# A fifth load buffer, loads in halves, a sum of squares in PSUM and branch products beside the last head in a one-core transformer block

## The chip, the cores and the metric

The kernel runs on one core of one Trainium2 chip. The metric is the device time of one execution in microseconds (us): for the kernel before, the median of three runs is 3460.16 us, from 3459.18 to 3461.2. The profile comes from one execution of 3459.31 us, whose span on the core is 3457.6 us.

Engine names: PE is TensorE (matmul), PEld its weight load, DVE VectorE, ACT ScalarE, POOL GpSimd, SP SyncE, which here issues DMAs.

## The reference, cut to what matters

One layer for 512 tokens (plus 16 meta tokens) of width 2048, in float32:

```
h  = rmsnorm(x)
x += (sigmoid(gate_a) * (MLA(h) @ w_a) + sigmoid(gate_b) * (StickBreaking(h) @ w_b)) @ w_out
x += PEER(rmsnorm(x))       # 128 x 128 experts, 8 heads, 16 experts a head and token
out = rmsnorm(x)
PEER, for one token:  act = gate * gelu(u[idx] . x);   y = sum over idx of act * v[idx]
```

MLA and stick-breaking have eight heads of width 128 each. The expert tables u and v have 16384 rows of 2048.

## The kernel before, in words

**Products.** A float32 product is made of three matmuls of split operands (`mm3`, L258 to L261): low weight by high value, high weight by low value, high by high. A weight block of 128 x 1024 goes through `wtile` (L232): SP loads it to a raw tile `wr` (L243), ACT copies it to `wh` (L245), DVE subtracts to get `wl` (L246), then 24 matmuls use both. Values are split the same way by `split` (L263): ACT copies (L264), DVE subtracts (L265). There are 4 raw buffers (`raw_half`, L229) and 3 pairs of `wh` and `wl`, in the output stage a fourth pair in a pool of its own (`weights_v`). A raw buffer is free again when its block's subtraction has ended, a pair when the block's matmuls have.

**Stages.** The front projections and stick-breaking attention fill the first 800 us. Then come the MLA heads, about 800 to 961 us: for each head h, generators are run in turn (`run`, L787), one step of each at a time: scores and softmax of head h+1 (`mla_s`, L724), projections of head h+2 (`mla_p`, L708) and the value product of head h (`mla_y`, L760). In `mla_y`, PE transposes the probabilities `pt` (L772), ACT and DVE split the transposes into `th` and `tl_`, and PE multiplies them with the values (L781 to L783). Beside the last head, h = 7, there is nothing else to run. The branch merge follows (loop over 16 chunks m): for `wa` and for `wb` a block is loaded and multiplied into one PSUM bank (24 matmuls of 128 x 512), then gated by a sigmoid (L836, L837) and added. Before the loop, the stick-breaking result `yb` is split into `yh_b` and `yl_b`.

**PEER.** 328 of the 512 tokens (ND) are computed densely, over all experts; the other 184 gather rows of u and v with indirect DMAs from POOL, and DVE multiplies (L1065) and accumulates (L1073) these rows, one row instruction of 128 x 2048 each. The u stage runs from about 1550 to 2488 us, and its activations go to memory (`h_d`, `g_d`). The output stage runs from about 2488 to 3440 us: it multiplies 256 blocks of v (`vb`), 128 x 1024 each, with the gated activations. The experts form NG = 32 groups of GRP = 4. The work goes in 33 steps i (STEPS), the first of 5 blocks, then of 8 (the last of 3); a step uses the groups i-1 and i. qi counts the blocks within a step.

**Activations of a group** arrive by two loads on SP, `hin` (L1327, 656 KB) and `gin` (L1319, 672 KB); each tile tag has two buffers. `gated` (L1333) multiplies them on DVE (L1337, L1339), at qi = QM = 3 of the step before they are used; `group_split` (L1406) splits the product into `vah` (ACT) and `val` (DVE, L265), at qi = 5 (4 in step 0). Right behind the split, `group_in` (L1324) issues both loads for the group after the next. SP takes its instructions in order; so a load whose buffer isn't free holds up the loads of weights behind it.

**What sets the order.** Each engine runs its instructions in the order in which the program gives them, after a scheduler that places them by their dependencies. By `follows` (L1330) the gated product stays behind the newest weight subtraction; the row instructions are spread by a pace (L1502).

**The end.** As each of the 16 chunks c of the output is complete (accumulated at L1498 and L1500), `fin_add` (L1417) squares it on ACT (L1420) and adds the square to `ssf` on DVE (L1422). `fin_out` (L1424) then sums over partitions by one matmul with ones (L301), makes 1/sqrt of it (`rstd`, L309 to L315: ACT ln, DVE scale, ACT exp, four DVE instructions), scales the 16 chunks (L1429) and issues 8 output DMAs (L1431). It is called once for the columns past 328, in the last step, and once at the very end for the first 328.

Of the kernel before, what the change touches and what calls it, by code (L numbers as in the profile page):

```python
# [2 lines left out]

# [20 lines left out]
P = 128  # L24
# [27 lines left out]
QM, QS = 3, 5  # L52
# [163 lines left out]
def body(tc, nc, a, dbg=None):  # L216
# [12 lines left out]
    def raw_half():  # L229
        return wp.tile([P, 1024], F32, name="wr", tag="wr", bufs=4)  # L230
# [568 lines left out]
    run(mla_s(0), mla_p(1))  # L799
    for h in range(H):  # L800
        if h == 1:
            mla_r(1)
        if h in (2, 3):
            mla_rope(h)
        if h == 4:
            values(1)
        run(*([mla_s(h + 1)] if h + 1 < H else []), *([mla_p(h + 2)] if h + 2 < H else []), mla_y(h))
# [18 lines left out]
    for m in range(KC):  # L826
        acc = []
        for name, yh_, yl_, gi in (("wa", *ys[0], 0), ("wb", *ys[1], 1)):
            gt = sp2.tile([P, SEQ], F32, name="g2", bufs=4)
            SP.dma_start(gt, gates[gi, m])  # L830
            wh, wl = front(name, m)
            ps = ps_tile()
            for k in range(8):
                s = slice(k * P, (k + 1) * P)
                mm3(ps, wh[:, s], wl[:, s], yh_[:, k], yl_[:, k], k == 0, k == 7)
# [479 lines left out]

    def group_g(g):
        gt = vi.tile([P, D], F32, name="gin", tag="gin")[:, :NBT * GRP * TH]
        gt = gt.rearrange("p (b j t) -> p b j t", j=GRP, t=TH)
        SP.dma_start(gt, g_d[g])  # L1319
        return gt  # L1320
# [3 lines left out]
    def group_in(g):  # L1324
        if g not in held:
            ht = hin_tile()
            SP.dma_start(ht, h_d[g])  # L1327
            held[g] = [ht, group_g(g)]

# [85 lines left out]
    rf = ap2.tile([P, SEQ], F32, name="rf")  # L1415

    def fin_add(c, t0, t1, first):  # L1417
        t = slice(t0, t1)
        sq = ssf if first else vp.tile([P, SEQ], F32, name="fsq", bufs=1)
        S.activation(sq[:, t], acc[:, c, t], AF.Square)  # L1420
        if not first:
            V.tensor_add(ssf[:, t], ssf[:, t], sq[:, t])  # L1422

    def fin_out(t0, t1):  # L1424
        sc = vp.tile([P, D], F32, name="sc", tag="row", bufs=1).rearrange("p (k t) -> p k t", t=SEQ)
        rstd(rf[:, t0:t1], ssf[:, t0:t1], t1 - t0, D, [sc[:, k] for k in range(3)], None)
        for c0, n in ((0, 1), (1, 2), (3, 3), (6, 3), (9, 3), (12, 2), (14, 1), (15, 1)):
# [3 lines left out]
            SP.dma_start(a["out"][c0:c0 + n, :, t0:t1].rearrange("k p t -> p k t"), acc[:, c0:c0 + n, t0:t1])  # L1431

# [8 lines left out]
    for i, step in enumerate(STEPS):  # L1441
# [11 lines left out]
        for qi, (g, q8) in enumerate(step):  # L1453
            wh, wl = wtile(a["vb"][at])
            at += 1
            if i + 1 < NG and qi == QM:
                gated(*held[i + 1])
# [21 lines left out]
            if i + 1 < NG and qi == (QS if i else 4):  # L1479
                group_split(i + 1)  # L1480
                if i + 2 < NG:
                    group_in(i + 2)
            for dc in range(2):
# [20 lines left out]
                if i >= NG - 1 and not stays:  # L1504
                    fin_add(c, 0, ND, not done)
# [4 lines left out]
    fin_out(0, ND)  # L1510
# [19 lines left out]
```

## Time and profile before

| what | value |
|---|---|
| time, median of three runs | 3460.16 us (3459.18 to 3461.2) |
| time of the profiled execution | 3459.31 us |
| its span on the core | 3457.6 us |
| PE busy | 3420.5 us, 99% |
| PEld busy | 3188.2 us, 92% |
| DVE busy | 2573.5 us, 74% |
| ACT busy | 1427.4 us, 41% |
| POOL busy | 776.1 us, 22% |
| moved by DMA | 919.94 MB, mean 266 GB/s |
| mean granted TensorE clock | 0.995 |

Busy shares are averages over stages of different kinds. A matmul's shown duration is longer than its share of the time, since matmuls are pipelined: how long one takes in a stream is read from the count in a window. "[1.79 <-DVE wl L246]" behind a row of a timeline says that the engine stood idle for 1.79 us before this instruction and that the last thing it waited for was the DVE instruction of L246 that wrote `wl`. In the table by windows, the clock is the share of full speed that was granted to TensorE, and the DMA share is the mean busy share of the core's 16 DMA engines.

### The profile page before, as it was taken

The numbers are of one execution on the slowest core, as the hardware profiler recorded it, in microseconds if no ns is written. First come the engines' busy times: TensorE is split into PE (matmuls) and PEld (weight loads), VectorE is DVE, ScalarE is ACT, GpSimd is POOL, SyncE is SP. The second block draws the span as 40 slices with busy tenths as digits, with TensorE's granted clock in tenths as the row PEclk, the third lists the DMA queues.
The fourth block names the chain that finished last, engine by engine and source line by source line (L and its number), as shares of the span: only waits on it lengthen the run. The fifth ranks groups of instructions, "written<-read, shape, count | busy, mean of one in ns | idle before, by whom it ended". The sixth has DMA issues, their size and how long they took to land.

```text
span 3457.6 us, 53380 instructions
## 1 busy us (share of the span) xinstructions
PE 3420.5 (99%) x21115; PEld 3188.2 (92%) x21115; DVE 2573.5 (74%) x3573; ACT 1427.4 (41%) x2304; POOL 776.1 (22%) x555
## 2 busy tenths in 40 slices
PE   9999999999999999999999999999999999999997
PEld 8988888887888888889999999999999999999997
DVE  5533334445754557999999988887889999999997
ACT  4233333334543223223576776774333333333333
POOL 1000000000001113322333333333213333333320
PEclk9999999999999999999999999999999999999998
DMA  5322323232144345559999999999999999999993
GB/s 171 100 98 100 98 100 100 89 101 74 62 131 143 129 143 181 204 214 367 377 389 407 405 412 412 405 401 398 403 362 375 394 408 400 402 382 399 409 381 116
DMA packets 227141, 919.94 MB, mean 266 GB/s; under 512 B 27806, under 2 KB 53518, under 8 KB 179090
## 3 DMA queue, kind: packets, MB, share of 16 engines
q1 hardware_dynamic: 134660, 466.11, 36.6%
q0 software_dynamic: 60480, 411.68, 30.0%
q10 hardware_dynamic: 31750, 38.75, 3.1%
q8 instruction: 165, 2.70, 0.3%
q14 instruction: 86, 0.70, 0.1%
HBM read 854.57 MB, written 62.91 MB: 265 GB/s over the span
## 4 chain that ended last, share of the span: by engine, by line
PE 81%; DVE 11%; DMA 4%; issue 2%; ACT 1%; SPq 0%; POOL 0%; DVEq 0%; ACTq 0%
PE ps L259 26%; PE ps L260 25%; PE ps L261 25%; DMA wr<-vb 3%; DVE wl L246 3%; DVE xg L1073 1%; DVE row L1065 1%; PE ps L1252 1%; DVE acc L1073 1%; DVE acc L1500 1%; DVE hgl L246 0%; ACT wh L245 0%; DVE hin L1337 0%; DMA row<-u,eo 0%; DVE acc L1429 0%
## 5 line engine op out<-in xcount | busy, mean ns | idle before, releaser
L245 ACT ACTIVATE wh<-wr 128x1024 fp32r<-128x1024 f32 (+1 forms) x654 | 687.8, 1053 | 1402.6 <-PE ps L261 1038.7
L246 DVE TENSOR_TENSOR wl<-wr,wh 128x1024 fp32r<-128x1024 f32 (+1 forms) x639 | 812.0, 1279 | 391.5 <-ACT wh L245 389.3
L259 PE MATMUL ps<-vah,wl 128*128 128x328 f32 x2048 | 643.8, 314 | 7.0 <-DVE wl L246 6.8
L260 PE MATMUL ps<-val,wh 128*128 128x328 f32 x2048 | 642.7, 314 | 0.0
L261 PE MATMUL ps<-vah,wh 128*128 128x328 f32 x2048 | 639.7, 312 | 0.0
L259 PE MATMUL ps<-hgh,wl 128*128 128x328 f32 (+1 forms) x1488 | 490.9, 330 | 2.8 <-DVE wl L246 2.8
L261 PE MATMUL ps<-hgh,wh 128*128 128x328 f32 (+1 forms) x1488 | 486.1, 327 | 0.0
L260 PE MATMUL ps<-hgl,wh 128*128 128x328 f32 (+1 forms) x1488 | 485.8, 326 | 0.0
L259 PE MATMUL ps<-xh,wl 128*128 128x512 f32 (+1 forms) x1376 | 468.1, 340 | 1.5 <-ACT xh L366 1.5
L260 PE MATMUL ps<-xl,wh 128*128 128x512 f32 (+1 forms) x1376 | 465.0, 338 | 0.8 <-DVE xl L367 0.8
L261 PE MATMUL ps<-xh,wh 128*128 128x512 f32 (+1 forms) x1376 | 464.9, 338 | 0.0
L259 PEld LDWEIGHTS ps<-vah,wl 128*128 128x128 f32 x2048 | 386.3, 189 | 9.5 <-DVE wl L246 9.3
L260 PEld LDWEIGHTS ps<-val,wh 128*128 128x128 f32 x2048 | 387.1, 189 | 0.0
L261 PEld LDWEIGHTS ps<-vah,wh 128*128 128x128 f32 x2048 | 386.8, 189 | 0.0
L1052 POOL DMA_INDIRECT row<-v,eo x128 | 215.5, 1684 | 481.4 <-DVE xg L1073 414.4
L1073 DVE SCALAR_TENSOR_TENSOR xg<-row,act,xg 128x2048 f32<-128x2048 f32 x127 | 297.5, 2343 | 1.2 <-DMA row<-v,eo 1.1
L1065 DVE SCALAR_TENSOR_TENSOR row<-row,xg 128x2048 f32<-128x2048 f32 x128 | 292.1, 2282 | 4.8 <-DMA row<-u,eo 4.8
L259 PEld LDWEIGHTS ps<-hgh,wl 128*128 128x128 f32 x1488 | 280.1, 188 | 14.6 <-DVE wl L246 3.4
L261 PEld LDWEIGHTS ps<-hgh,wh 128*128 128x128 f32 x1488 | 280.1, 188 | 11.7 <-issue 0.2
L260 PEld LDWEIGHTS ps<-hgl,wh 128*128 128x128 f32 x1488 | 280.4, 188 | 10.9
L259 PEld LDWEIGHTS ps<-xh,wl 128*128 128x128 f32 x1376 | 258.6, 188 | 30.2 <-ACT xh L366 3.0
L260 PEld LDWEIGHTS ps<-xl,wh 128*128 128x128 f32 x1376 | 259.1, 188 | 29.1 <-DVE xl L367 1.7
(517 smaller groups left out, 6057.6 us busy)
## 6 DMA issues: line engine op xcount, KB each, us to landing
wr<-ut SPq DMA_DIRECT2D x256, 512.0 KB, 9.4
wr<-vb SPq DMA_DIRECT2D x256, 512.0 KB, 8.0
wr<-front SPq DMA_DIRECT2D x238, 512.0 KB, 3.3
g_d<-gb POOLq DMA_DIRECT2D x42, 512.0 KB, 10.9
gin<-g_d SPq DMA_DIRECT2D x32, 672.0 KB, 7.4
h_d<-hb ACTq DMA_DIRECT2D x128, 164.0 KB, 8.3
hin<-h_d SPq DMA_DIRECT2D x32, 656.0 KB, 8.9
gates<-gt ACTq DMA_DIRECT2D x32, 256.0 KB, 2.0
```

Source lines behind the costliest of these rows:

```text
L245: more["last"] = S.activation(hi[:, s], r, AF.Copy)
L246: sub = (eng or V).tensor_sub(lo[:, s], r, hi[:, s].bitcast(F32))
L259: T.matmul(ps, wl, xh, start=start, stop=False)
L260: T.matmul(ps, wh, xl, start=False, stop=False)
L261: T.matmul(ps, wh, xh, start=False, stop=stop)
L1052: G.indirect_dma_start(out=row, out_offset=None, in_=a[src], in_offset=bass.IndirectOffsetOnAxis(ap=eos[part][:, k:k + 1], axis=0))
L1065: ins = V.scalar_tensor_tensor(row, row, 1.0, xs[part], ALU.mult, ALU.mult, accum_out=w)
L1073: ins = V.scalar_tensor_tensor(y, row, w, y, ALU.mult, ALU.add)
L1252: T.matmul(bank[:, o:o + P], ohs[q % 4][:, 1, :, t], wos[:, q % 4, c, :, t], start=c == 1, stop=c == 0)
L1500: mark = V.tensor_add(acc[:, c, :ND], acc[:, c, :ND], ps[:, :ND])
```

## The change

Four parts.

- **A fifth raw buffer** in the output stage: every fifth `wr` tile comes from the pool `weights_v`. Room is made by putting `rf` into a fourth part of the scratch tile `sc`, and by making the tile of squares 328 wide, in two buffers, rather than 512 wide in one.
- **Activation loads in four halves.** Groups 0 and 1 are loaded as before. For groups from 2 on, `group_part` issues one of four loads at each of the blocks qi = 0 to 3 (1 to 4 in step 1) of the step before the group is used: two of `hin` (two of the four experts each, 128 x 656) and two of `gin` (128 x 640 and 128 x 704). The gated product is at qi = 3, 5, 4 in steps 0, 1 and from 2 on, the split at 4, 6, 5. Whole loads for the group after the next, behind the split, are gone.
- **The last square in PSUM.** `fin_last` sums, in one PSUM bank, `ssf` of the first 15 chunks and then the square of the last chunk, by two matmuls with ones; `fin_end` makes the root with three DVE instructions behind the exp rather than four, and sends the output by 10 DMAs rather than 8.
- **Branch products beside the last heads.** `branch_ahead` splits `yb` into tiles of its own (8 splits, beside head 6) and makes the `wb` products for m = 0, 1, 2 beside heads 6 and 7, two k at a step. The merge loop takes these banks when it comes to them. The splits into `yh_b` and `yl_b` stay as well.

```diff
-QM, QS = 3, 5
+QM, QS = 4, 5
...
     def raw_half():
+        if more["pool"] is not None and more["n"] % 5 == 0:
+            return more["pool"].tile([P, 1024], F32, name="wr", tag="wr")
         return wp.tile([P, 1024], F32, name="wr", tag="wr", bufs=4)
 
...
+    AHEAD = 3
+    ready = {}
+
+    def branch_ahead():
+        bh, bl = ([lp.tile([P, 4, n], F32R, name=x, tag=t)[:, :, :SEQ] for t, n in ((f"cq{p}", SEQ), (f"ck{p}", LEN))]
+                  for x, p in (("ybh", "h"), ("ybl", "l")))
+        for h in range(H):
+            split(bh[h // 4][:, h % 4], bl[h // 4][:, h % 4], yb[:, h])
+            yield
+        for m in range(AHEAD):
+            wh, wl = front("wb", m)
+            ps = ready[m] = ps_tile()
+            for k in range(8):
+                s = slice(k * P, (k + 1) * P)
+                mm3(ps, wh[:, s], wl[:, s], bh[k // 4][:, k % 4], bl[k // 4][:, k % 4], k == 0, k == 7)
+                if k % 2:
+                    yield
+
...
-        run(*([mla_s(h + 1)] if h + 1 < H else []), *([mla_p(h + 2)] if h + 2 < H else []), mla_y(h))
+        if h == H - 2:
+            ahead = branch_ahead()
+        run(*([mla_s(h + 1)] if h + 1 < H else []), *([mla_p(h + 2)] if h + 2 < H else []), mla_y(h),
+            *([ahead] if h == H - 1 else [islice(ahead, 9)] if h == H - 2 else []))
...
-            wh, wl = front(name, m)
-            ps = ps_tile()
-            for k in range(8):
-                s = slice(k * P, (k + 1) * P)
-                mm3(ps, wh[:, s], wl[:, s], yh_[:, k], yl_[:, k], k == 0, k == 7)
+            if gi and m in ready:
+                ps = ready.pop(m)
+            else:
+                wh, wl = front(name, m)
+                ps = ps_tile()
+                for k in range(8):
+                    s = slice(k * P, (k + 1) * P)
+                    mm3(ps, wh[:, s], wl[:, s], yh_[:, k], yl_[:, k], k == 0, k == 7)
...
+    def group_part(g, k):
+        if k == 0:
+            held[g] = [hin_tile(), gin_tile()]
+        ht, gt = held[g]
+        j, b = slice(k * GRP // 2, (k + 1) * GRP // 2), slice((k - 2) * NBT // 2, (k - 1) * NBT // 2)
+        ld = SP.dma_start(ht[:, j], h_d[g][:, j]) if k < 2 else SP.dma_start(gt[:, b], g_d[g][:, b])
+        tc.add_manual_dep(ld.ins, more["last"].ins.name, NOSYNC, reason="keeps the loads spread")
 
...
-    rf = ap2.tile([P, SEQ], F32, name="rf")
 
     def fin_add(c, t0, t1, first):
         t = slice(t0, t1)
-        sq = ssf if first else vp.tile([P, SEQ], F32, name="fsq", bufs=1)
-        S.activation(sq[:, t], acc[:, c, t], AF.Square)
+        sq = ssf[:, t] if first else vp.tile([P, ND], F32, name="fsq", bufs=2)[:, :t1 - t0]
+        S.activation(sq, acc[:, c, t], AF.Square)
         if not first:
-            V.tensor_add(ssf[:, t], ssf[:, t], sq[:, t])
+            V.tensor_add(ssf[:, t], ssf[:, t], sq)
 
...
+        rf = sc[:, 3]
...
+    final = {}
+
+    def fin_last(c):
+        ps = final["ps"] = ps_tile()
+        T.matmul(ps[:, :ND], ones, ssf[:, :ND], start=True, stop=False)
+        sq = vp.tile([P, ND], F32, name="fsq", bufs=2)
+        S.activation(sq, acc[:, c, :ND], AF.Square)
+        T.matmul(ps[:, :ND], ones, sq, start=False, stop=True)
+
+    def fin_end():
+        sc = vp.tile([P, D], F32, name="sc", tag="row", bufs=1).rearrange("p (k t) -> p k t", t=SEQ)
+        v, r0, t, rf = (sc[:, k, :ND] for k in range(4))
+        ps = final["ps"][:, :ND]
+        S.activation(t, ps, AF.Ln, scale=1.0 / D, bias=C("eps"))
+        V.tensor_scalar(v, ps, 1.0 / D, EPS, ALU.mult, ALU.add)
+        S.activation(r0, t, AF.Exp, scale=-0.5)
+        V.tensor_mul(v, v, r0)
+        V.scalar_tensor_tensor(v, v, -0.5, r0, ALU.mult, ALU.mult)
+        V.scalar_tensor_tensor(rf, v, 1.5, r0, ALU.add, ALU.mult)
+        for c0, n in ((0, 1), (1, 1), (2, 2), (4, 2), (6, 2), (8, 2), (10, 2), (12, 2), (14, 1), (15, 1)):
+            for c in range(c0, c0 + n):
+                V.scalar_tensor_tensor(acc[:, c, :ND], acc[:, c, :ND], gain("fin")[:, c:c + 1],
+                                       rf, ALU.mult, ALU.mult)
+            SP.dma_start(a["out"][c0:c0 + n, :, :ND].rearrange("k p t -> p k t"), acc[:, c0:c0 + n, :ND])
 
...
-            if i + 1 < NG and qi == QM:
+            if 1 <= i < NG - 1:
+                for k in ({k + (i == 1): (k,) for k in range(4)}).get(qi, ()):
+                    group_part(i + 1, k)
+            if i + 1 < NG and qi == (3, 5, QM)[min(i, 2)]:
                 gated(*held[i + 1])
...
-            if i + 1 < NG and qi == (QS if i else 4):
+            if i + 1 < NG and qi == (4, 6, QS)[min(i, 2)]:
                 group_split(i + 1)
-                if i + 2 < NG:
-                    group_in(i + 2)
...
-                    fin_add(c, 0, ND, not done)
+                    if len(done) == KC - 1:
+                        fin_last(c)
+                    else:
+                        fin_add(c, 0, ND, not done)
                     done.append(c)
...
-    fin_out(0, ND)
+    fin_end()
```

How it moves instructions, at three places. Line numbers of the changed kernel differ: L249 is the weight subtraction there (L246 before), L1365 the load of a half, L1375 and L1377 the gated product, L1562 and L1564 the accumulation, L1100 the row instruction, L268 the split on DVE.

First SP's queue at the start of the output stage, where the loads of `vb` blocks (`wr`) begin. Before:

```order
145 L243 DMA wr<-vb 128x1024 x7
146 L1395 DMA select<-select 128x56
147 L243 DMA wr<-vb 128x1024
148 L1319 DMA gin<-g_d 128x1344
149 L243 DMA wr<-vb 128x1024
150 L1327 DMA hin<-h_d 128x1312
151 L243 DMA wr<-vb 128x1024 x4
152 L1319 DMA gin<-g_d 128x1344
153 L243 DMA wr<-vb 128x1024 x2
154 L1327 DMA hin<-h_d 128x1312
155 L243 DMA wr<-vb 128x1024
156 L1327 DMA hin<-h_d 128x1312
```

And of the changed kernel:

```order
143 L246 DMA wr<-vb 128x1024 x7
144 L1433 DMA select<-select 128x56
145 L246 DMA wr<-vb 128x1024 x3
146 L1365 DMA hin<-h_d 128x656 x2
147 L1365 DMA gin<-g_d 128x640
148 L246 DMA wr<-vb 128x1024 x3
149 L1365 DMA gin<-g_d 128x704
150 L246 DMA wr<-vb 128x1024 x4
151 L1365 DMA hin<-h_d 128x656 x2
152 L246 DMA wr<-vb 128x1024
153 L1365 DMA gin<-g_d 128x640
154 L246 DMA wr<-vb 128x1024
```

Seven weight loads come before `select` in both. Behind it, one weight load and then a whole `gin` and `hin` stood between the blocks, each with one block; now three weight loads come first, and the halves stand between them.

Second, DVE at the same place, from the first subtractions for `vb` blocks (`wl`) on. Before:

```order
2036 L246 TENSOR_TENSOR wl<-wr,wh 128x1024 x4
2037 L1498 COPY acc<-ps 128x328
2038 L1071 TENSOR_SCALAR acc<-row,actb 128x16x128
2039 L1498 COPY acc<-ps 128x328
2040 L1337 TENSOR_TENSOR hin<-hin,gin 128x20x4x16
2041 L1498 COPY acc<-ps 128x328
2042 L1339 TENSOR_TENSOR hin<-hin,gin 128x4x8
2043 L246 TENSOR_TENSOR wl<-wr,wh 128x1024
2044 L1498 COPY acc<-ps 128x328
2045 L1073 SCALAR_TENSOR_TENSOR acc<-row,actb,acc 128x16x128
2046 L1498 COPY acc<-ps 128x328 x2
2047 L1073 SCALAR_TENSOR_TENSOR acc<-row,actb,acc 128x16x128
```

And of the changed kernel:

```order
2041 L249 TENSOR_TENSOR wl<-wr,wh 128x1024 x3
2042 L1562 COPY acc<-ps 128x328
2043 L1098 TENSOR_SCALAR acc<-row,actb 128x16x128
2044 L1562 COPY acc<-ps 128x328
2045 L249 TENSOR_TENSOR wl<-wr,wh 128x1024
2046 L1562 COPY acc<-ps 128x328
2047 L249 TENSOR_TENSOR wl<-wr,wh 128x1024
2048 L1562 COPY acc<-ps 128x328
2049 L1100 SCALAR_TENSOR_TENSOR acc<-row,actb,acc 128x16x128
2050 L1562 COPY acc<-ps 128x328
2051 L1375 TENSOR_TENSOR hin<-hin,gin 128x20x4x16
2052 L1562 COPY acc<-ps 128x328
```

Four subtractions stood ahead of the first accumulation, and one more behind the gated product (L1337, L1339); now three stand ahead, two more follow between accumulations, and then comes the gated product.

Third, DVE in a later step of the output stage, from one of its subtractions on. Before:

```order
2083 L246 TENSOR_TENSOR wl<-wr,wh 128x1024
2084 L1500 TENSOR_TENSOR acc<-acc,ps 128x328
2085 L1073 SCALAR_TENSOR_TENSOR xg<-row,act,xg 128x2048
2086 L246 TENSOR_TENSOR wl<-wr,wh 128x1024 x4
2087 L1337 TENSOR_TENSOR hin<-hin,gin 128x20x4x16
2088 L1339 TENSOR_TENSOR hin<-hin,gin 128x4x8
2089 L246 TENSOR_TENSOR wl<-wr,wh 128x1024
2090 L1500 TENSOR_TENSOR acc<-acc,ps 128x328
2091 L1073 SCALAR_TENSOR_TENSOR xg<-row,act,xg 128x2048
2092 L1500 TENSOR_TENSOR acc<-acc,ps 128x328
2093 L1073 SCALAR_TENSOR_TENSOR xg<-row,act,xg 128x2048
2094 L246 TENSOR_TENSOR wl<-wr,wh 128x1024
```

And of the changed kernel:

```order
2089 L249 TENSOR_TENSOR wl<-wr,wh 128x1024
2090 L1100 SCALAR_TENSOR_TENSOR xg<-row,act,xg 128x2048
2091 L249 TENSOR_TENSOR wl<-wr,wh 128x1024 x5
2092 L1564 TENSOR_TENSOR acc<-acc,ps 128x328
2093 L1100 SCALAR_TENSOR_TENSOR xg<-row,act,xg 128x2048
2094 L1564 TENSOR_TENSOR acc<-acc,ps 128x328
2095 L1100 SCALAR_TENSOR_TENSOR xg<-row,act,xg 128x2048
2096 L1375 TENSOR_TENSOR hin<-hin,gin 128x20x4x16
2097 L1564 TENSOR_TENSOR acc<-acc,ps 128x328
2098 L1377 TENSOR_TENSOR hin<-hin,gin 128x4x8
2099 L1100 SCALAR_TENSOR_TENSOR xg<-row,act,xg 128x2048
2100 L1564 TENSOR_TENSOR acc<-acc,ps 128x328
```

Four subtractions in a row were followed by the gated product and a fifth; now five stand in a row, and the gated product comes later, among row instructions and accumulations.

More of the change, by code (lines that the diff above doesn't have):

```diff
@@ L2 @@
 from contextlib import ExitStack
+from itertools import islice
 import numpy as np
@@ L1313, in body, with gin_tile @@
     steps, gate_steps = routing(), gating()
+    def gin_tile():
+        gt = vi.tile([P, D], F32, name="gin", tag="gin")[:, :NBT * GRP * TH]
+        return gt.rearrange("p (b j t) -> p b j t", j=GRP, t=TH)
     def group_g(g):
-        gt = vi.tile([P, D], F32, name="gin", tag="gin")[:, :NBT * GRP * TH]
-        gt = gt.rearrange("p (b j t) -> p b j t", j=GRP, t=TH)
+        gt = gin_tile()
         SP.dma_start(gt, g_d[g])
```

## The prediction

> **What bounds the kernel now.** I read the page's first part, then PE by windows. PE is busy almost without a break; so only places where it stands idle or runs at a lower clock can pay, and the path to the end behind its last product.
>
> ```profile
> span 3457.6 us, 53380 instructions
> PE 3420.5 (99%) x21115; PEld 3188.2 (92%) x21115; DVE 2573.5 (74%) x3573; ACT 1427.4 (41%) x2304; POOL 776.1 (22%) x555
> ```
>
> The table by windows (busy time and count of each engine, clock, DMA share, GB/s), for the MLA heads and the output stage; the short windows are right behind two long gaps of PE:
>
> ```profile
> 800.00:960.00 160.00, 155.08 (x893) 130.65 (x891) 110.89 (x276) 87.71 (x202) 11.53 (x15) 0.99 0.19 58
> 2500.00:2600.00 100.00, 94.58 (x604) 93.30 (x602) 83.78 (x70) 28.72 (x28) 20.47 (x16) 0.97 0.95 364
> 2600.00:3300.00 700.00, 698.91 (x4657) 697.90 (x4656) 654.87 (x558) 232.85 (x216) 233.58 (x133) 1.00 1.00 396
> 2800.00:2900.00 100.00, 99.05 (x660) 98.78 (x660) 94.83 (x80) 33.69 (x32) 30.39 (x21) 1.00 1.01 397
> 2530.70:2534.10 3.40, 3.40 (x14) 3.40 (x14) 3.40 (x3) 0.00 (x0) 0.94 (x1) 0.50 0.96 384
> 2559.00:2562.00 3.00, 3.00 (x21) 3.00 (x22) 3.00 (x4) 0.00 (x0) 1.28 (x2) 1.00 1.02 406
> 2564.80:2568.20 3.40, 3.40 (x14) 3.40 (x14) 3.40 (x4) 0.00 (x0) 0.94 (x1) 0.50 0.99 411
> ```
>
> In 2600 to 3300 PE makes 4657 matmuls in 698.91 us, 0.15 us each, so a block of 24 takes 3.6 us and a step of 8 blocks 28.8 us. Nothing is to be had there from PE; but DVE is busy for 654.87 of 700 us and the DMA share is 1.00. The loss sits in 2500 to 2600: 604 matmuls against 100 / 0.15 = 667, and 63 x 0.15 = 9.45 us.
>
> The timeline of PE names the gaps (idle time in brackets):
>
> ```profile
> 2506.74 0.42 PE L259 MATMUL ps<-vah,wl 128*128 128x328 f32 x1 [0.50 <-DVE wl L246]
> 2530.44 0.46 PE L259 MATMUL ps<-vah,wl 128*128 128x328 f32 x1 [1.79 <-DVE wl L246]
> 2558.88 0.42 PE L259 MATMUL ps<-vah,wl 128*128 128x328 f32 x1 [1.34 <-DVE wl L246]
> 2564.52 0.42 PE L259 MATMUL ps<-vah,wl 128*128 128x328 f32 x1 [1.79 <-DVE wl L246]
> 2863.24 0.42 PE L259 MATMUL ps<-vah,wl 128*128 128x328 f32 x1 [0.95 <-DVE wl L246]
> ```
>
> The first four are 5.42 us of idle time. Behind both gaps of 1.79 us, and not behind the one of 1.34, the clock was 0.50 for 3.4 us: 14 matmuls, worth 14 x 0.15 = 2.1 us, so 1.3 us lost each. The rest of the 9.45, 1.4 us, I spread over the four gaps as slow starts, about 0.35 each.
>
> Why `wl` is late, from the timelines of SP, DVE and ACT:
>
> ```profile
> 2495.97 0.35 SPq L243 DMA_DIRECT2D wr<-vb  x1
> 2503.31 0.33 SPq L1327 DMA_DIRECT2D hin<-h_d  x1
> 2506.71 3.73 SPq L243 DMA_DIRECT2D wr<-vb  x4
> 2494.73 1.21 DVE L246 TENSOR_TENSOR wl<-wr,wh 128x1024 fp32r<-128x1024 f32 x1
> 2501.77 1.52 DVE L265 TENSOR_TENSOR val<-hin,vah 128x1312 fp32r<-128x1312 f32 x1
> 2505.47 4.62 DVE L246 TENSOR_TENSOR wl<-wr,wh 128x1024 fp32r<-128x1024 f32 x4
> 2515.96 1.06 ACT L245 ACTIVATE wh<-wr 128x1024 fp32r<-128x1024 f32 x1 [8.62 <-DMA wr<-vb]
> 2539.95 1.06 ACT L245 ACTIVATE wh<-wr 128x1024 fp32r<-128x1024 f32 x1 [10.18 <-DMA wr<-vb]
> ```
>
> Between the subtractions at 2494.73 and 2505.47 no raw buffer came free, so SP had no weight load to issue from 2495.97 to 2506.71; `hin` waited for the split that ended at 2503.29. The load issued at 2506.71 let ACT start at 2515.96, 9.3 us later. The gaps at 2530, 2558 and 2564 come from that: loads issued late, then DVE behind.
>
> **Part by part.**
>
> *Fifth buffer and halves, the late gaps.* One more raw buffer lets each weight load go one block, 3.6 us, earlier; the halves go out at the head of a step into tiles that the step before freed, so no load stands behind a split. The gaps of 1.79, 1.34 and 1.79 us are less than 3.6; I take all three as gone. With their slow starts and both clock drops they are 9.45 - 0.50 - 0.35 = 8.6 us.
>
> *The first gap grows.* In the new order one more subtraction (the fourth) falls into the full stretch of DVE that ends at 2505.47. It costs 4.62 / 4 = 1.155 us, so the gap becomes 0.50 + 1.155 = 1.65 us. That lies between 1.34 (no drop) and 1.79 (drop), nearer to the drop, so I count one: 1.65 + 0.35 + 1.3 = 3.3 us in place of 0.85; without a drop 2.0.
>
> The Trainium skill (TensorE: Matmul & The Clock Gate, § Why this matters for your kernels) warns only of idle gaps over about 3 us; by it the new gap would cost no drop, and the sum would be 1.3 us lower. The rows at 2530.70 and 2564.80 disagree with it, and the measurement decides.
>
> Together the two parts give -8.6 + (3.3 - 0.85) = -6.1 us; bounds -7.4 (no drop) and -2 (the later gaps only halved: -4.3 + 2.4).
>
> *The gap at 2863.24.* 660 matmuls against 667 are 1.05 us. It comes of DVE being late for one `wl`; the next load is earlier but the order changes too. Half: -0.5, bounds 0 and -1.05.
>
> *Cost on queues.* SP issues four loads a step where it issued two, 0.35 us each by the rows above, beside eight weight loads: 12 x 0.35 = 4.2 us of a step of 28.8. SP waits most of the time, so nothing.
>
> ```profile
> wr<-vb SPq DMA_DIRECT2D x256, 512.0 KB, 8.0
> gin<-g_d SPq DMA_DIRECT2D x32, 672.0 KB, 7.4
> hin<-h_d SPq DMA_DIRECT2D x32, 656.0 KB, 8.9
> ```
>
> The bytes stay the same, and time to landing hardly follows size (512 KB 8.0 us, 672 KB 7.4): it is time in a full queue. The last half goes out beside the load of block 3, and DVE comes to the gated product only behind block 4's subtraction and, in the new order, two row instructions and two accumulations; so nothing for late halves either.
>
> New small gaps I allow for with +1.4 us, about one and a half of the size of that at 2863; bounds 0 and +5.
>
> *The end.* The chain behind the last product, by the timeline:
>
> ```profile
> 3439.12 0.31 PE L261 MATMUL ps<-vah,wh 128*128 128x328 f32 x1
> 3439.69 0.50 DVE L1422 TENSOR_TENSOR ssf<-ssf,fsq 128x328 f32<-128x328 f32 x1 [0.54 <-ACT fsq L1420]
> 3440.11 0.49 DVE L1500 TENSOR_TENSOR acc<-acc,ps 128x328 f32<-128x328 f32 x1
> 3441.20 0.50 DVE L1422 TENSOR_TENSOR ssf<-ssf,fsq 128x328 f32<-128x328 f32 x1 [0.60 <-ACT fsq L1420]
> 3441.76 1.22 PE L301 MATMUL ps<-ssf,cst 128*128 128x328 f32 x2 [2.32 <-DVE ssf L1422]
> 3444.08 0.50 DVE L312 TENSOR_TENSOR sc<-sc 128x328 f32<-128x328 f32 x1
> 3445.15 0.33 DVE L314 TENSOR_SCALAR sc<-sc 128x328 f32<-128x328 f32 x1
> 3446.05 1.03 DVE L1429 SCALAR_TENSOR_TENSOR acc<-acc,gn,rf 128x328 f32<-128x328 f32 x2
> 3442.00:3457.60 15.60, 0.97 (x2) 0.05 (x1) 9.95 (x21) 1.01 (x2) 0.00 (x0) 0.50 0.47 172
> ```
>
> The addition at 3441.20 goes from the path: -0.5. The one at 3439.69 stands ahead of the last accumulation (3440.11), though the product had ended by 3439.5; with the chunk before finished earlier by the second buffer of squares, -0.4. The sum of 1.22 us runs at a clock of 0.50 (last row); it comes about 0.9 us earlier and follows the first matmul of its pair, so I take full clock, 0.6 us: -0.6, or 0 if the clock has already dropped. From L312 to the first L1429 were 3446.05 - 3444.08 = 1.97 us for four instructions; three of 0.53 are 1.6: -0.4. The last output load is issued behind the last scaling as before. Sum -1.9; bounds -1.3 and -2.3.
>
> *Branch products.* PE waits at the last heads:
>
> ```profile
> 951.07 0.30 PE L772 MATMUL ps<-cst,pt 128*128 128x128 f32 x1 [0.53 <-DVE pt L755]
> 959.74 0.41 PE L772 MATMUL ps<-cst,pt 128*128 128x128 f32 x2 [1.01 <-DVE pt L755]
> 960.73 0.50 PE L781 MATMUL ps<-th,vnl 128*128 128x512 f32 x1 [0.58 <-ACT th L264]
> 950.84 0.68 DVE L265 TENSOR_TENSOR yal<-ps,yah 128x512 fp32r<-128x512 f32 x1
> ```
>
> That is 2.1 us of gaps, at most about 2.6 with slow starts. 72 matmuls move beside the last heads; they lie on PE either way, so only gaps that they fill count. Ahead of the last wait for `pt` stand 13 of them; even at the 328-wide rate of 0.15 us they are 2.0 us, more than 1.01. Against that, DVE and ACT get 8 more splits (0.68 us each on DVE, 5.4 us), most of them beside head 6, in a stretch where DVE is busy for 110.89 of 160 us; part of them delays the scores' chain. The splits into `yh_b` are not saved. I take -1.0; bounds -2.6 and +1.5.
>
> **Sum.** -6.1 - 0.5 + 1.4 - 1.9 - 1.0 = -8.1 us; against the profiled execution, 3459.31 - 8.1 = 3451.2. The median of the runs is 0.85 higher, 3460.16, and the forecast for it is 3452.0. A measurement of this kernel can tell about 0.2%, 6.9 us, from no change: faster means under 3453.2.
>
> **Rivals.**
>
> *The late loads stay.* If DVE, not the buffers, sets when `wl` comes, the three later gaps are only halved (-2 in place of -6.1), and the sum is -4: 3456. For it speaks that DVE is 83.78 busy even in the window with the loss; against it the ACT rows, which wait 8.62 and 10.18 us for the DMA. Chance 0.25, no measurable change.
>
> *All gaps go.* No drop behind the first gap, none at 2863, branch gaps filled, no new ones: -7.4 - 1.05 - 2.3 - 2.6 = -13.4, 3447. Chance 0.2.
>
> *DVE becomes the bound, slower.* Five subtractions now stand in a row, and then four accumulations, three row instructions and the gated product without one. By the lines of DVE in 2600 to 3300 a row instruction takes 2.34 us:
>
> ```profile
> L1073 DVE SCALAR_TENSOR_TENSOR xg<-row,act,xg 128x2048 f32<-128x2048 f32 x102 | 238.9, 2342 | 0.0
> ```
>
> That makes 3 x 2.34 + 4 x 0.49 = 9.0 us and the gated product. The fifth needs a pair of `wh` and `wl` which PE frees only at the end of a block, so DVE, which takes its queue in order, can stand idle with row instructions and accumulations behind it. DVE's spare time is (700 - 654.87) / 700 x 28.8 = 1.86 us a step. It decides at 1.86 us of such idle time a step; at 2.4 us each of 30 steps would lose 0.54, 16 us in all, and with the gains of the rest (-8.1) the kernel takes about 3468. Against it: four in a row were there already, and PE was idle for only 700 - 698.91 = 1.09 us in 2600 to 3300. Chance 0.09.
>
> *More transfers cost DMA time, slower.* The DMA share is 1.00, so any fixed time a transfer holds the engines is paid in landings. The landings above spread by 1.5 us without order of size, so a fixed part of that size can't be excluded. A third of it, 0.5 us for each of two more transfers, would be 1 us a step; PE would feel it when the fifth buffer's 3.6 us are used up, after which it costs up to 30 us less 8: 3482. Against it speaks that 672 KB land sooner than 512 KB. Chance 0.03.
> The Trainium skill (SBUF — State Buffer, § The DMA setup-cost knee) states a roughly fixed 2 us for every transfer and the rule to make each as large as can be; if none of it overlapped, that would be 4 us a step. No row here shows a fixed part apart from the queue.
>
> **How the numbers follow.** The forecast's own case, -6 to -11, has 0.43; most of that, 0.35, lies below 3453.2. Faster: 0.35 + 0.2 = 0.55. Same: 0.25 + 0.08 = 0.33. Slower, past 3467: 0.12. The range 3444 to 3464 holds the forecast, the case of all gaps gone with its bounds and the case of late loads with its allowance for new gaps at +5; left out are the slower cases and little more.
>
> **What would show it.** In the changed profile: 2500 to 2600 with 645 or more matmuls; one gap of about 1.65 us near 2507, with a clock of 0.50 behind it; no `wh` waiting 8 us or more for `wr` there; DVE idle before its subtractions no longer than before in 2600 to 3300; about 5.0 us from the last product to the first scaling of the end (3446.05 - 3439.12 = 6.93 before), the sum at full clock; about 1 us of PE gaps at the last two heads. Wrong would be: gaps in most steps behind five subtractions, landings of `wr` much over 8.0 us, or later gaps still in place.

## The result and the profile after

The changed kernel takes 3479.92 us (median of six runs, 3478.36 to 3484.18), the kernel before 3460.68 us in the same comparison. The ratio is 1.0058, with a 95% interval from 1.0046 to 1.0071: slower by some 20 us (16 to 25), where 8 us faster was forecast. The span of the profiled execution went from 3457.6 to 3478.8 us, 21.2 us more. The page's first part, of the changed kernel:

```profile
span 3478.8 us, 53527 instructions
PE 3434.5 (99%) x21117; PEld 3200.7 (92%) x21117; DVE 2577.7 (74%) x3579; ACT 1430.4 (41%) x2312; POOL 767.3 (22%) x555
```

DVE's work is the same, 2577.7 us against 2573.5. So something waits that did not wait before. The table by windows says where:

```profile
2500.00:2600.00 100.00, 97.53 (x641) 97.26 (x640) 88.85 (x76) 32.08 (x30) 30.63 (x17) 0.98 0.97 373
2600.00:3300.00 700.00, 685.01 (x4492) 681.42 (x4491) 633.75 (x536) 221.98 (x207) 214.00 (x130) 0.98 0.97 380
3300.00:3400.00 100.00, 96.53 (x626) 96.27 (x626) 87.98 (x75) 32.82 (x31) 25.30 (x15) 0.97 0.93 370
```

The start of the output stage is better: 641 matmuls against 604. But 2600 to 3300, where PE had been busy for 698.91 us, now has 4492 against 4657: 165 x 0.15 = 24.8 us lost. In 3300 to 3400 there are 626; the kernel before has 670 there, in this row:

```profile
3300.00:3400.00 100.00, 100.00 (x670) 100.00 (x669) 89.38 (x79) 33.43 (x33) 23.30 (x14) 0.98 0.81 310
```

That is 44 x 0.15 = 6.6 us more. In 2600 to 3300 the DMA share fell from 1.00 to 0.97, so the loss does not come of more work for the DMA engines.

The waits of PE and of DVE in the output stage (total us, times, longest), first PE's in the kernel before, then those of the changed kernel:

```profile
PE ps L259 <- DVE wl L246: 6.8, 6, 1.8
PE ps L262 <- DVE wl L249: 20.8, 14, 4.4
DVE hin L1375 <- DMA gin<-g_d: 31.0, 10, 7.1
DVE hin L1375 <- issue: 7.4, 3, 2.7
```

The gated product (L1375) now waits on DVE for `gin`, 38.4 us in 13 of its 32 times. In the kernel before there was one such wait, of 2.0 us. The worst one, by the timelines of SP, DVE and PE:

```profile
3195.03 0.42 SPq L1365 DMA_DIRECT2D gin<-g_d  x1
3201.59 1.23 DVE L249 TENSOR_TENSOR wl<-wr,wh 128x1024 fp32r<-128x1024 f32 x1 [0.18 <-ACT wh L248]
3202.74 0.49 DVE L1564 TENSOR_TENSOR acc<-acc,ps 128x328 f32<-128x328 f32 x1
3210.37 1.49 DVE L1375 TENSOR_TENSOR hin<-hin,gin 128x1280 f32<-128x1280 f32 x1 [7.15 <-DMA gin<-g_d]
3222.78 1.22 DVE L249 TENSOR_TENSOR wl<-wr,wh 128x1024 fp32r<-128x1024 f32 x1
3224.05 0.64 PE L262 MATMUL ps<-vah,wl 128*128 128x328 f32 x1 [4.35 <-DVE wl L249]
3224.50:3227.90 3.40, 3.40 (x14) 3.40 (x14) 3.40 (x3) 0.00 (x0) 1.24 (x2) 0.50 0.98 365
```

The last half of `gin` is issued at 3195.03. A subtraction ends at 3202.8, one accumulation follows, and then DVE stands for 7.15 us until the half is there, 15.3 us after its issue. Everything behind it in DVE's queue is that much later: a subtraction, row instructions, accumulations, the split, and above all the subtraction at 3222.78. It ends at 3224.0, and PE, which had stood for 4.35 us, starts at 3224.05. Behind that gap the clock is 0.50 (last row). The other gaps have the same start: between 2600 and 3400 PE stands nine times for 0.6 us or more, and each time DVE had waited ahead of the last gated product before it.

How early the loads of one group were issued before, by two rows of SP and one of DVE:

```profile
2642.89 0.33 SPq L1319 DMA_DIRECT2D gin<-g_d  x1
2648.63 0.45 SPq L1327 DMA_DIRECT2D hin<-h_d  x1
2697.17 1.48 DVE L1337 TENSOR_TENSOR hin<-hin,gin 128x1280 f32<-128x1280 f32 x1
```

In the kernel before both loads went out as soon as their buffers were free (`gin` behind a gated product, `hin` behind a split), 48.5 us ahead of their use. I matched the loads with the 30 gated products of groups 2 to 31, in the order of the two queues, and took the time from the issue of the last load to where DVE was free for the product. This lead has a median of 48.4 us before and of 10.8 us after, with 11 of 30 under 10 us. The issues and times to landing after:

```profile
wr<-vb SPq DMA_DIRECT2D x256, 512.0 KB, 8.9
hin<-h_d SPq DMA_DIRECT2D x60, 328.0 KB, 6.9
gin<-g_d SPq DMA_DIRECT2D x30, 352.0 KB, 9.7
gin<-g_d SPq DMA_DIRECT2D x30, 320.0 KB, 7.9
```

The trace shows the landings of about a third of the halves: medians of 7 to 10 us, in two cases 14.8 and 15.2, against a lead of 10.8. That is the theory to be tested.

### The profile page after: what moved, and what is told of

It reads as the page before. It is cut to its first block, busy times and chain, and to the rows that moved or that the text cites. A ratio compares the mean times of both kernels' runs of the same rounds, so it can differ in the third digit from the quotient of the medians.

```text
span 3478.8 us, 53527 instructions
## 1 busy us (share of the span) xinstructions
PE 3434.5 (99%) x21117; PEld 3200.7 (92%) x21117; DVE 2577.7 (74%) x3579; ACT 1430.4 (41%) x2312; POOL 767.3 (22%) x555
## 4 chain that ended last, share of the span: by engine, by line
PE 75%; DVE 14%; DMA 6%; issue 4%; ACT 1%; SPq 0%; POOL 0%; DVEq 0%; ACTq 0%; POOLq 0%
PE ps L262 24%; PE ps L263 24%; PE ps L264 24%; DMA gin<-g_d 3%; DVE wl L249 3%; DVE xg L1100 2%; DVE row L1092 2%; PE ps L1279 1%; DVE acc L1564 1%; DMA wr<-vb 1%; DVE xgb L1100 1%; DVE acc L1100 1%; DMA hin<-h_d 1%; DVE hgl L249 1%; DVE val L268 0%
## 5 line engine op out<-in xcount | busy, mean ns | idle before, releaser
L249 DVE TENSOR_TENSOR wl<-wr,wh 128x1024 fp32r<-128x1024 f32 (+1 forms) x639 | 811.2, 1277 | 372.3 <-ACT wh L248 368.7
L262 PEld LDWEIGHTS ps<-vah,wl 128*128 128x128 f32 x2048 | 390.0, 190 | 25.0 <-DVE wl L249 24.9
L1100 DVE SCALAR_TENSOR_TENSOR xg<-row,act,xg 128x2048 f32<-128x2048 f32 x127 | 297.7, 2344 | 2.1 <-DMA row<-v,eo 2.1
```

Source lines behind the costliest of these rows:

```text
L249: sub = (eng or V).tensor_sub(lo[:, s], r, hi[:, s].bitcast(F32))
L262: T.matmul(ps, wl, xh, start=start, stop=False)
L1100: ins = V.scalar_tensor_tensor(y, row, w, y, ALU.mult, ALU.add)
```

## The experiments

**Theory A**: the last half is issued too late against the gated product; DVE waits for it, and its queue with it. **Rival B**: the fifth buffer does it. **Rival C**: the row of five subtractions and the long pause behind it, by the order alone, as the prediction's slower rival had it. **Rival D**: four transfers a step cost DMA time that two don't. A fourth suspicion, that part of the loss is in the branch products or the end, has its own kernel. All ratios are to the kernel before, on the same chip, with 95% intervals; in the experiments it took 3458.5 to 3458.8 us. "Stage" is the time from the first to the last product of a `vb` block in the profiled execution; "lead" the median worked out as above; "DVE wait" the idle time of DVE right before all gated products. Lead, wait and stage come from one execution each, while the time is a median; the runs of a kernel differ by 6 to 23 us, so a difference of a few us in the stage can be chance.

| kernel | lead us | DVE wait us | stage us | time us | ratio |
|---|---|---|---|---|---|
| before | 48.4 | 2.0 | 951.1 | 3460.7 | 1 |
| changed | 10.8 | 38.4 | 977.6 | 3479.9 | 1.0058 (1.0046 to 1.0071) |
| whole_loads | 48.4 | 2.5 | 948.9 | 3454.4 | 0.9989 (0.9979 to 0.9998) |
| halves_old_place | 24.9 | 1.8 | 950.3 | 3454.0 | 0.9983 (0.9974 to 0.9992) |
| halves_early | 17.3 | 1.3 | 952.0 | 3462.3 | 1.0012 (1.0003 to 1.0021) |
| gated_later | 13.9 | 3.3 | 955.2 | 3457.3 | 0.9997 (0.9988 to 1.0005) |
| whole_late | 10.7 | 39.7 | 983.1 | 3481.6 | 1.0061 (1.0045 to 1.0076) |
| gated_sooner | 4.2 | 166.8 | 1078.8 | 3582.6 | 1.0358 (1.0342 to 1.0374) |
| four_buffers | 11.9 | 16.7 | 1001.9 | 3504.8 | 1.0137 (1.0123 to 1.0152) |

**The old loads** (whole_loads). The changed kernel with this edit:

```diff
-QM, QS = 4, 5
+QM, QS = 3, 5
-            if 1 <= i < NG - 1:
-                ...
-                    group_part(i + 1, k)
-            if i + 1 < NG and qi == (3, 5, QM)[min(i, 2)]:
+            if i + 1 < NG and qi == QM:
...
-            if i + 1 < NG and qi == (4, 6, QS)[min(i, 2)]:
+            if i + 1 < NG and qi == (QS if i else 4):
                 group_split(i + 1)
+                if i + 2 < NG:
+                    group_in(i + 2)
```

> The changed kernel with the old activation loads: a whole hin and a whole gin behind the split, gated product and split at their old blocks; fifth raw buffer, end and branch products stay. Theory A (the gated product waits for a half that was issued too late, and DVE's whole queue waits behind it): the 31 us of DVE idle time ahead of the gated product go, and the output stage comes back from 977 us to 951 or less, 3453 us or below in all. Rival B (the fifth buffer itself does it, since more weight loads stand in the DMA queue): still 3470 to 3480.

Measured: 3454.43 us, ratio 0.9989, 1.4 us above what was expected; the stage came back as expected, to 948.9 us. The window 2600 to 3300 is full again:

```profile
2600.00:3300.00 700.00, 700.00 (x4665) 700.00 (x4665) 657.11 (x557) 232.81 (x216) 228.82 (x133) 1.00 1.00 397
```

The loss is in the loads, with the gated product and the order that go with them; rival B falls, since the fifth buffer is there.

**One load buffer less** (four_buffers).

```diff
-        if more["pool"] is not None and more["n"] % 5 == 0:
-            return more["pool"].tile([P, 1024], F32, name="wr", tag="wr")
```

> The changed kernel without the fifth raw buffer; halves stay. Theory A: the last half is issued as late as before against the gated product, so DVE still waits there; and with one weight load less ahead nothing covers the waits of PE: as slow as the changed kernel or slower, 3478 to 3500. Rival B (the fifth buffer does it): back to 3455 to 3462.

Measured: 3504.76 us, slower still, above what I had expected. So with the halves the fifth buffer saves 25 us. But DVE waits only 16.7 us for the gated product here; the rest must be something else, and the last group of experiments takes it up.

**The gated product one block later, or one sooner** (gated_later, gated_sooner); halves and buffers stay.

```diff
-            if i + 1 < NG and qi == (3, 5, QM)[min(i, 2)]:
+            if i + 1 < NG and qi == (3, 5, 5)[min(i, 2)]:      # sooner: (3, 5, 3)
...
-            if i + 1 < NG and qi == (4, 6, QS)[min(i, 2)]:
+            if i + 1 < NG and qi == (4, 6, 6)[min(i, 2)]:      # sooner: (4, 6, 4)
```

> The changed kernel with the gated product at block 5 and the split at block 6 in steps from 2 on, one block later; five buffers, four halves and five subtractions in a row stay. Theory A: one block gives the halves 3.6 us more, against DVE waits of 1.2 to 7.2 us: idle time ahead of the gated product falls from 38 us to under 8, and the time to 3452 to 3460. Rival C (five subtractions in a row, then none for 10 us): no change, 3475 to 3485. Rival D (four transfers a step cost DMA time): no change, and weight loads still wait.

> The changed kernel with the gated product at block 3 and the split at block 4, one block sooner; halves and buffers as they are. Theory A: 3.6 us less for the last half, so the wait, 38 us in 13 steps before, comes in most of 30 steps with 3 to 5 us each, 90 to 150 us in all, of which DVE's spare time of 1.9 us a step covers 55 at most; 3510 to 3570. Rival C (the row of five subtractions): here it is four, then the gated product, then one, as in the kernel before, so 3452 to 3460.

Measured: 3457.27 us later, 3582.61 us sooner. Rows of five subtractions are still there with the later product (in 7 steps, 8 in the changed kernel), and with the sooner one they are rows of four but for one, as in the kernel before; so rival C has both the wrong way round. The waits of DVE, in the kernel with the sooner product:

```profile
DVE hin L1375 <- DMA gin<-g_d: 140.9, 24, 9.2
DVE hin L1375 <- issue: 17.4, 3, 7.1
DVE hin L1375 <- DMA wr<-vb: 8.5, 1, 8.5
```

Together 166.8 us, and the stage is 127.7 us longer than before. With 38.4 us of such waits it was 26.5 us longer. That is 0.77 and 0.69 us of the stage for each us of DVE's wait; I take the rest to be covered by DVE's spare time, which is argued and not shown. The sooner product went past my range of 3510 to 3570, since waits of up to 9.2 us came where I had taken 3 to 5.

**The halves two blocks earlier** (halves_early): two beside block 0 and two beside block 1.

```diff
-                for k in ({k + (i == 1): (k,) for k in range(4)}).get(qi, ()):
+                for k in {i == 1: (0, 1), 1 + (i == 1): (2, 3)}.get(qi, ()):
```

> The changed kernel with the same four halves a step, but two beside each of the first two blocks rather than one beside each of four; gated product and split at their places. Theory A: the last half goes out two blocks (7.2 us) earlier, DVE's waits ahead of the gated product go nearly all: 3450 to 3458. Rival C: the order of subtractions is nearly the same, 3475 to 3485. Rival D (number of transfers): 3475 to 3485; and bunched loads could push weight loads back, with waits of ACT for wr over 10 us.

Measured: 3462.26 us, with hardly a wait ahead of the gated product (1.3 us in all). The earlier issue took most of the loss away, from 1.0058 to 1.0012. DVE's subtractions stand in the same rows here as in the changed kernel, eight of them of five; so of all these kernels this one moves the lead most nearly alone. It is not as good as the kernels with the old place, and 4 us above my range. Its profile still has five gaps of PE of 0.7 to 4.6 us; where those come from was not followed up, and the profiled execution, of 3455.41 us, is the fastest of its runs, 7 us below their median, so what the median has more of is not shown.

**Whole loads at late places** (whole_late): `hin` beside block 1, `gin` beside block 3. **Halves at the old place** (halves_old_place): four back to back behind the split. In place of the loop over `group_part` (`paced` ties a load to the newest copy of ACT, as `group_part` does):

```diff
+                if qi == 1 + (i == 1):
+                    held[i + 1] = [hin_tile(), None]
+                    paced(SP.dma_start(held[i + 1][0], h_d[i + 1]))
+                if qi == 3 + (i == 1):
+                    held[i + 1][1] = gin_tile()
+                    paced(SP.dma_start(held[i + 1][1], g_d[i + 1]))
```

And of whole_loads, behind the split:

```diff
-                    group_in(i + 2)
+                    for k in range(4):
+                        group_part(i + 2, k)
```

> The changed kernel with two whole loads a step instead of four halves, at late places: hin beside block 1, gin beside block 3 of the step before the group is used; gated product at block 4, five buffers. Theory A (what counts is when the last bytes are issued against the gated product, not into how many pieces they are cut): DVE waits ahead of the gated product as in the changed kernel or more, 3475 to 3495. Rival D (four transfers cost DMA time where two don't): 3452 to 3460.

> Four halves back to back at the old place, behind the split, for the group after the next; gated product and split at their old blocks; five buffers. Theory A: the same as with whole loads there, 3451 to 3458. Rival D (number of transfers): 3470 or more.

Measured: 3481.64 and 3454.03 us. Two transfers at the late places are as slow as four; four at the old place are as fast as two, though their lead is 24.9 us and not 48.4. Rival D falls. The wait of DVE in the kernel with whole loads at late places is that of the changed kernel:

```profile
DVE hin L1378 <- DMA gin<-g_d: 39.7, 13, 5.5
```

**Only the end and the branch products** (ends_only): the changed kernel with the old loads and four raw buffers, both edits from above.

> Only the end and the branch products changed: four raw buffers, whole loads and the old order of the output stage. Expected from the traces of the changed kernel: the path behind the last product 2.2 us shorter, the branch products 0.9 us, the output stage's gaps as before: about 3 us less than the kernel before, 3455 to 3457. A rival that puts part of the loss on the branch products would see it here as no gain or a loss.

Measured: 3455.37 us, ratio 0.9988 (0.9978 to 0.9998). That is 3.3 us less than the kernel before, by the interval 1 to 8, where 2.9 were forecast for these two parts; none of the loss is theirs.

**What the fifth buffer is worth, and why four buffers with halves are so slow** (four_later, four_old_halves), and the lead of both remedies together (early_and_later). The edits are those of four_buffers with gated_later, of four_buffers with halves_old_place, and of halves_early with gated_later.

> Four raw buffers, four halves beside blocks 0 to 3, gated product one block later. With four raw buffers the kernel lost 50 us in the output stage though DVE waited only 16.7 us for halves. If those 50 us are waits of the subtractions for weight loads (five in a row with four raw buffers: the fifth load can only be issued when the first subtraction has ended), the loss stays for the most part: 3475 to 3500. If they still come from the halves, it goes: 3452 to 3462.

> Four raw buffers, four halves back to back at the old place behind the split, old blocks of the gated product and the split. Tells what the fifth buffer is worth where the activation loads are early. The prediction gave it over 6 us; if so, this takes 3459 or more. With whole loads the profiles with four and with five buffers differ by 3 us in the output stage, which says 3453 to 3458.

> Five buffers, halves beside blocks 0 and 1, gated product at block 5 and split at block 6: the last half has some 21 us instead of 11. Theory A: DVE waits ahead of the gated product are nil and the time is 3452 to 3458, no better than one of the two alone, since either already took the waits away.

Measured: 3492.45 us, ratio 1.0090 (1.0065 to 1.0114); 3458.77 us, ratio 0.9997 (0.9989 to 1.0006); 3453.38 us, ratio 0.9987 (0.9978 to 0.9996). The second is 0.8 us above the range from the profiles, and just short of what the prediction's worth of the fifth buffer called for. With four buffers and the later product DVE waits only 0.2 us for `gin`, and the kernel is slow all the same. Its waits are these, of ACT and of DVE:

```profile
ACT wh L246 <- DMA wr<-vb: 351.0, 116, 9.3
DVE wl L247 <- ACT wh L246: 97.4, 43, 5.9
DVE hin L1373 <- DMA gin<-g_d: 0.2, 1, 0.2
```

And the same of the changed kernel, with five, and of four_old_halves, with four:

```profile
ACT wh L248 <- DMA wr<-vb: 54.0, 19, 6.2
DVE wl L249 <- ACT wh L248: 42.7, 31, 4.7
ACT wh L246 <- DMA wr<-vb: 263.0, 91, 9.4
DVE wl L247 <- ACT wh L246: 59.6, 41, 4.4
```

So here the subtractions wait for weight loads. The wait of ACT alone doesn't price it, since four_old_halves has 263.0 us of it and is as fast as the kernel before; what differs more is DVE's wait, 97.4 against 59.6 us. A possible reason is that five subtractions stand in a row, while with four raw buffers the load for the fifth goes out only when the first has ended. But of DVE's idle time ahead of its subtractions in four_later only about a third stands ahead of the fourth and fifth of a row of five. Whether those rows or the place of the halves among the weight loads does it was not tried apart, so rival C stays open for four buffers; for five it is wrong. Where the activation loads are early, the fifth buffer's worth is small: with halves at the old place 3454.03 against 3458.77 us, in different comparisons (0.9983 and 0.9997, the intervals just overlap), with whole loads 3454.43 against 3455.37, no difference.

The early and later kernel has the shortest stage of all, 947.0 us, but its time is that of halves_old_place and whole_loads within the intervals. These three and ends_only are some 0.1 to 0.2% ahead of the kernel before, by intervals that just exclude no change.

## Why the prediction was wrong, point by point

**The step that failed** is the one on queues: a half goes out beside block 3, DVE comes to the gated product only behind block 4's subtraction, two row instructions and two accumulations, "so nothing for late halves either". It gave no time for this. By the prediction's own rows those five instructions take 1.16 + 2 x 2.34 + 2 x 0.49 = 6.8 us, less than the 7.4 and 8.9 us to landing that it printed above them. And the order that it named is that of one step. In the changed trace two accumulations and two row instructions stand between the last subtraction and the gated product in 12 of the 30 groups; their lead has a median of 12.4 us, and one of them waits, 1.2 us. In the other 18 fewer stand there, in 17 of them one or none; the median lead is 9.4 us, and 12 of them wait, 37.2 us together. One of each kind, first without a wait:

```profile
2598.55 1.23 DVE L249 TENSOR_TENSOR wl<-wr,wh 128x1024 fp32r<-128x1024 f32 x1 [2.43 <-ACT wh L248]
2599.69 0.49 DVE L1564 TENSOR_TENSOR acc<-acc,ps 128x328 f32<-128x328 f32 x1
2600.10 2.35 DVE L1100 SCALAR_TENSOR_TENSOR xg<-row,act,xg 128x2048 f32<-128x2048 f32 x1
2602.36 0.49 DVE L1564 TENSOR_TENSOR acc<-acc,ps 128x328 f32<-128x328 f32 x1
2602.77 2.35 DVE L1100 SCALAR_TENSOR_TENSOR xg<-row,act,xg 128x2048 f32<-128x2048 f32 x1
2605.03 1.49 DVE L1375 TENSOR_TENSOR hin<-hin,gin 128x1280 f32<-128x1280 f32 x1
```

The other is the product at 3210.37, shown above, with one accumulation in between. Leads of 10.8 us in the middle and 5.7 at least stand against times to landing with medians of 7 to 10 us, and a wait comes from the late ones: one half took 15.2 us. And the halves were priced by what they cost on SP; what the old loads had, 48 us of lead, was never worked out, though the timelines of SP and DVE before show it.

**A wait at DVE** then holds up work that has nothing to do with the half. ACT, whose split needs the product too, stood 87.4 us for it against 30.8 before; how much of the loss goes by ACT's queue was not tried apart, but halves_early has 59.4 us of that wait without the loss. The prediction named the queue behind the fifth subtraction as the slower rival, with 0.09 and 3468 us. The engine and the way to PE were right, the cause not: in the changed kernel none of the 13 waits for `gin` follows a row of five, and halves_early, with the same rows, is within 1 us of the stage before.

**The late gaps at the start** went by the number forecast. PE's gaps there, in the changed kernel, are down to one:

```profile
2505.70 0.64 PE L262 MATMUL ps<-vah,wl 128*128 128x328 f32 x1 [2.47 <-DVE wl L249]
```

It is the first gap, which the prediction let grow to 1.65 us with a clock drop; it grew to 2.47, and the drop came. The gap grew by 1.97 us where one more subtraction, 1.155, was counted; where the rest comes from was not followed up. The window 2500 to 2600 gained 37 matmuls, 5.6 us, where 6.1 were forecast. The forecast gave this to the fifth buffer and the halves together; the buffer's part isn't borne out. In 2490 to 2600 there are 671 matmuls before and 707 in the changed kernel; here are whole_loads, with five buffers, and four_old_halves, with four:

```profile
2490.00:2600.00 110.00, 104.83 (x669) 104.29 (x668) 94.86 (x82) 34.83 (x33) 26.78 (x19) 0.95 0.95 373
2490.00:2600.00 110.00, 108.01 (x709) 106.12 (x708) 96.52 (x83) 34.37 (x32) 23.86 (x19) 1.00 0.96 372
```

Four buffers gain as much here, and five with whole loads nothing. So in these executions, one of each kernel, the fifth buffer is neither needed for the gain nor enough for it; what brings it stays open.

**The new small gaps**, an allowance of 1.4 us, are where the loss lands in the sum: the term measured 24.8 + 6.6 us, what PE lost in 2600 to 3400. Its larger gaps there come through the late halves, as said above.

**The end** gained 2.2 us where 1.9 were forecast: the span ends 16.2 us after the start of the last product, 18.4 before. Its timeline, last product to first scaling:

```profile
3462.60 0.31 PE L264 MATMUL ps<-vah,wh 128*128 128x328 f32 x1
3464.06 0.82 PE L1478 MATMUL ps<-fsq,cst 128*128 128x328 f32 x2 [0.44 <-ACT fsq L1477]
3465.48 0.50 DVE L1485 TENSOR_SCALAR sc<-ps 128x328 f32<-128x328 f32 x1 [2.04 <-ACT sc L1484]
3467.69 2.91 DVE L1492 SCALAR_TENSOR_TENSOR acc<-acc,gn,sc 128x328 f32<-128x328 f32 x6
```

From product to scaling are 5.09 us, 5.0 forecast. The second sum takes 0.82 us, less than 1.22 and more than the 0.6 of the forecast.

**The branch products** gained 0.9 us where 1.0 was forecast. A mark ahead of them, in an earlier head, and the first product behind the merge, of before:

```profile
906.07 0.44 PE L783 MATMUL ps<-tl__7495,vnh 128*128 128x384 f32 x1 [0.17 <-DVE tl__7495 L265]
1138.74 0.39 PE L259 MATMUL ps<-mgh,wl 128*128 128x512 f32 x1
```

And of the changed kernel:

```profile
904.39 0.44 PE L786 MATMUL ps<-tl__7495,vnh 128*128 128x384 f32 x1 [0.17 <-DVE tl__7495 L268]
1136.12 0.39 PE L262 MATMUL ps<-mgh,wl 128*128 128x512 f32 x1
```

Between the marks lie 232.67 us before and 231.73 after. All twelve profiles with the branch products, the changed kernel's among them, have 231.7 to 231.8. That the changed kernel is 1.7 us ahead at the first mark already is not the change, which has no instruction up to there; in those twelve profiles that mark lies anywhere from 903.8 to 906.2.

**The account**: -0.9 for the branch products, -2.1 in the rest of the time ahead of the output stage (1.7 of it ahead of the first mark, which the change doesn't explain), +26.5 in it (951.1 to 977.6), -2.2 at the end; 21.3 us, the difference of the spans.

**The rule on the clock.** The Trainium skill (TensorE: Matmul & The Clock Gate, § Why this matters for your kernels) warns of idle gaps over about 3 us. Here gaps of 2.47, 3.46, 3.87 and 4.35 us were followed by half clock, and the gap of 1.61 at 2769 was not; in the kernel before the two of 1.79 were. So a drop came behind shorter gaps than that rule has it. But no border shows: in the experiments gaps of 2.80 us (halves_early), 3.21 (four_later) and 3.45 (gated_sooner) were followed by full clock. The length of a gap alone does not decide, as the prediction took it to between 1.34 and 1.79; that its drop came is in part luck. The rows behind the gaps of 3.87 and of 1.61, of the changed kernel, and behind the one of 3.45:

```profile
2978.00:2981.40 3.40, 3.40 (x15) 3.40 (x14) 3.40 (x5) 0.00 (x0) 0.00 (x0) 0.50 0.99 413
2769.50:2772.90 3.40, 3.40 (x23) 3.40 (x24) 3.40 (x5) 1.06 (x1) 0.63 (x1) 1.00 1.02 379
2924.90:2928.30 3.40, 3.39 (x22) 3.39 (x23) 3.40 (x3) 0.00 (x0) 2.20 (x1) 1.00 0.93 313
```

**The rule on sizes.** The prediction cited the Trainium skill (SBUF — State Buffer, § The DMA setup-cost knee) for a fixed part of some 2 us in every transfer, so that large ones are better. Here 3454.03 us with four transfers a step and 3454.43 with two at their old places, and 3479.9 and 3481.6 at the late ones: in this stage, with a DMA share of 0.96 to 1.00, cutting a load in two cost nothing that could be measured.

## What to carry to other kernels

Before moving a load, work out from the trace the time between its issue and its use, and hold that against the spread of times to landing in that stage, not against their median. A wait of an engine that works in order costs what stands behind it in its queue; so the loads that such an engine waits for should have the longest lead of all, and cutting them into parts does not replace lead. An extra buffer is judged together with the order it allows: here it was worth 25 us with one order of loads, and nothing to 5 us with another.

## What the runs showed of the hardware that was not expected

The clock also drops without a gap. During and behind 32 small matmuls that sum gathered rows (L1534, 128 x 8, from 2622.48 to 2627.18) PE ran at half clock in the changed kernel, though the timeline has no idle time of PE there:

```profile
2626.00:2627.40 1.40, 1.40 (x7) 1.40 (x8) 0.18 (x1) 0.00 (x0) 0.27 (x1) 0.50 0.95 379
2627.50:2630.90 3.40, 3.40 (x14) 3.40 (x14) 3.40 (x3) 0.00 (x0) 0.00 (x0) 0.50 1.03 423
```

Before, no drop came at the same 32 matmuls (at 2631.30, 3.63 us), so it is not the small matmuls alone; what decides stays open.
